# Output projection in two halves of the tokens, in a decoder step on one Trainium2 core

## The chip, the core and the metric

The kernel runs on one core of a Trainium2 chip. The core has a matrix engine (TensorE, PE in the profile; PEld is its weight load), VectorE (DVE), ScalarE (ACT), GpSimd (POOL) and a queue engine that starts transfers (SyncE, SP). They run side by side and wait for each other by semaphores. SBUF is the working memory with 128 partitions, PSUM the memory of eight banks into which TensorE writes. The metric is the device time of one execution in microseconds (us).

## What is computed

One layer of a decoder trunk for 512 prompt tokens and 64 sample tokens (8 sequences of 8), 576 in all, with model width 2048, in float32. Cut to the part that matters here:

```python
h = modulate(rmsnorm(x, norm1_g), shift1, scale1)
proj = h @ w_in                       # five groups of 1024 columns
out_lru = rec * gelu(y_gate)          # recurrent branch
out_sc = sc_b * conv_out              # short convolution
mix = concat([rmsnorm(out_lru, gnorm_lru_g), rmsnorm(out_sc, gnorm_sc_g)]) @ w_out
x = x + gate1 * mix
h2 = modulate(rmsnorm(x, norm2_g), shift2, scale2)
x = x + gate2 * peer(h2)              # 8 heads; queries are h2 @ w_q, 256 columns each
y = rmsnorm(x, final_g)
```

shift, scale and gate come from `silu(c) @ w_ada + b_ada`. `peer` scores the queries against two sets of 128 keys, picks 16 of 16384 experts for each token and head, and sums the chosen rows.

## The kernel before

Activations lie transposed: 128 channels on the partitions, 16 slices of channels (`KD`), 576 tokens (`T`) along the free dimension. A float32 product is made of three: both operands are split into a high part (rounded to the matrix format) and a low part (the rest), and high by high, high by low and low by high are summed in PSUM (`mm3`, L132). The tokens are taken in two moving operands of 288 (`HT`): `movs[0]` holds the first 288 prompt tokens, `movs[1]` the other 224 and the 64 samples. `hv[0]` and `hv[1]` are the high and low parts of the activation.

A weight matrix of 128 output channels comes in two halves of eight slices (`half_w`, L123): a transfer of 512 KB, a copy on ACT that makes the high part, a subtraction that makes the low part. `lo_engine` (L114) gives the subtraction to POOL or VectorE in a fixed share of eighths; all calls before use 8 of 8, so POOL. High, low and raw tiles have two buffers each.

The order on TensorE is written out by hand (`manual_schedule`) through the first part of the kernel; the order on the other engines is planned when the kernel is built, by priority in order of the program and a model of durations.

The stages around the change: The short-convolution branch ends with `sc_b` for its last group; the first eight slices of the mix (recurrent branch) are split into `hv` already. `out_half(0, 0)` and `out_half(1, 0)` take the first eight slices for output tiles 0 and 1, with the second branch's norm statistics (`norm_stats`, `spread`) between and behind. VectorE then norms slices 8 to 15 (L607) and they are split. The loop over `k` (L618) makes the 16 output tiles: product, `x1 = gate * p + x` (L626 to L629, x loaded again as `xk`), a store of x1 to DRAM for the end of the kernel, the sum of squares (`square_sum`), and x1 times scale2 in place (L632, L633), which has to wait until the store has read x1. `ada_turn` puts pieces of the adaLN product (`ada_mm`, one 1 MB tile of `w_ada`, four buffers in `adap`, tag `wa`) between; `ada_out` transposes a finished group.

Behind the loop: the statistics of x1, their spread over partitions by a product (`R`), and for each quarter `q` of the channels `modulate` (L263), which makes h2 in high and low parts, the first query product `mm3(pq0, ...)` for these four slices, and a transposition of the prompt tokens of h2 by products with the identity into `wide`, copied by ACT and stored to `h2d` (L670). Then the other queries follow, with scores and top-16 selection.

PSUM: `pp` has two tiles of two banks (one bank for each token half of an output tile); `pa` and `pst` have two banks each. Behind the loop they are closed, and `ps2` and `psw` take the banks.

Of the kernel before, what the change touches and what calls it, by code (L numbers as in the profile page):

```python
# [81 lines left out]
def build(ctx, tc, A, O, dbg=None):  # L82
# [40 lines left out]
    def half_w(src, nm, hf, share=8):  # L123
        raw = ws.tile([128, 8, 128], F32, name=f"raw_{nm}_{hf}", tag="wraw", bufs=2)
        nc.sync.dma_start(raw, src[:, 8 * hf:8 * hf + 8, :])
        hi = ws.tile([128, 8, 128], F32R, name=f"whi_{nm}_{hf}", tag="whi", bufs=2)
        S.activation(hi, raw, AF.Copy)  # L127
        lo = ws.tile([128, 8, 128], F32R, name=f"wlo_{nm}_{hf}", tag="wlo", bufs=2)
        lo_engine(share).tensor_sub(lo, raw, r32(hi))  # L129
        return hi, lo  # L130

    def mm3(outs, his, los, movs, ks=range(KD)):  # L132

        for k in ks:
            wh, wl = his[k // 8][:, k % 8, :], los[k // 8][:, k % 8, :]
            for st, pick in ((wh, 0), (wh, 1), (wl, 0)):
                first = k == 0 and st is wh and pick == 0
                last = k == KD - 1 and st is wl
                for o, mv in zip(outs, movs):
                    PE.matmul(o, st, mv[pick](k), start=first, stop=last)  # L140
# [24 lines left out]
    pp = p1p.enter_context(tc.tile_pool(name="pp", bufs=2, space=PSUM))  # L165
# [452 lines left out]
    for k in range(KD):  # L618
        if k < 2:
            out_half(k, 1)  # L620
            p = p_out[k]
        else:
            p = project(A["w_out"][k], f"o{k}")
        xk = wk.tile([128, T], F32, name=f"xk{k}", tag="yg", bufs=2)
        nc.sync.dma_start(xk, A["xt"][:, k, :])
        V.scalar_tensor_tensor(x1[:, k, :HT], p[:, 0, :HT], g1[:, k, 0:1], xk[:, :HT], op0=ALU.mult, op1=ALU.add)  # L626
        V.scalar_tensor_tensor(x1[:, k, HT:NP], p[:, 1, :NX], g1[:, k, 0:1], xk[:, HT:NP], op0=ALU.mult, op1=ALU.add)
        V.tensor_tensor(s3(p[:, 1, NX:HT]), s3(p[:, 1, NX:HT]), ctx_b(g1, k), op=ALU.mult)
        V.tensor_add(x1[:, k, NP:], p[:, 1, NX:HT], xk[:, NP:])  # L629
        nc.sync.dma_start(x1d[:, k, :], x1[:, k, :])  # L630
        square_sum(x1[:, k, :], k, st, "n2")
        S.activation(x1[:, k, :NP], x1[:, k, :NP], AF.Copy, scale=mods[4][:, k, 0:1])  # L632
        V.tensor_tensor(s3(x1[:, k, NP:]), s3(x1[:, k, NP:]), ctx_b(mods[4], k), op=ALU.mult)  # L633
        ada_turn(1, 6)
    w_q = stream_w(A["wq"][0], "q00")
    ada_turn(2, 0)
    spread = norm_stats(st, D, "n2")
    ada_turn(1, 0)
    R = spread()
# [4 lines left out]
    psum["p"] = ctx.enter_context(tc.tile_pool(name="ps2", bufs=1, space=PSUM))

    def pbank(tag, nm, bufs):
        return psum["p"].tile([128, 512], F32, name=nm, tag=tag, bufs=bufs)

    psw = ExitStack()
    wp = psw.enter_context(tc.tile_pool(name="psw", bufs=1, space=PSUM))  # L650
# [3 lines left out]
    pq0 = [pbank("u", f"qa00{i}", 2)[:, :HT] for i in range(2)]  # L654
    for q in range(4):
        modulate(x1, R, None, 3, 4 * q, 4, "h2")
        mm3(pq0, *w_q, movs, range(4 * q, 4 * q + 4))
        t = adap.tile([128, 4, 512], F32, name=f"h2s{q}", tag="wa")
        for i in range(NA // 128):
            if i % 2 == 0:  # L660
                wide = wp.tile([128, 2, 512], F32, name=f"wide{q}{i}", tag="wide", bufs=2)
            for k in range(4):
                for p in range(2):
                    PE.matmul(wide[:, i % 2, k * 128:(k + 1) * 128], hv[p][:, 4 * q + k, i * 128:(i + 1) * 128], idr,
                              start=p == 0, stop=p == 1)
            if i % 2:
                with tc.high_priority():
                    S.activation(t[:, i - 1:i + 1, :], wide, AF.Copy)
        for i in range(NA // 128):
# [1272 lines left out]
```

## Time and profile before

| | us |
|---|---|
| three executions | 3202.97, 3201.39, 3187.74 (median 3201.39) |
| the profiled execution | 3192.57 |
| its span, first to last instruction | 3190.7 |
| granted TensorE clock in it, mean | 0.984 of full |
| output projection, densest part | 723.4 to 910.2 us of the span |
| from its last product to the end of the first query product and the turning of h2 | 910.2 to 963.5 us |

The page gives busy times of engines over the span. A row of the timeline gives a start, a duration, the engine, the line, the operation, what is written and read, and in brackets how long the engine sat idle before and who ended that. A row of the windows gives for a stretch the busy time of PE, PEld, DVE, ACT and POOL with instruction counts, the granted clock, and the share and rate of the DMA engines. The first number of a row of a group is its count, then busy us and mean ns.

### The profile page before, as it was taken

What the parts mean: (1) busy time and instruction counts of PE and PEld (TensorE: products, weight loads), DVE (VectorE), ACT (ScalarE), POOL (GpSimd) and SP (SyncE); (2) the same over time, 40 slices, a digit from 0 to 9 for tenths busy, and PEclk for the clock granted to TensorE, in tenths of its full rate; (3) what the DMA queues carried; (4) which work ended last, traced back from release to release, by engine and by line L of the source; (5) the groups of instructions that cost most, each with busy time, mean ns of one, the idle gap of its engine ahead of it and who ended that gap; (6) DMA issues with size and microseconds to landing.
All of it is one profiled execution on the core that took longest, in us unless ns stands there. A gap on an engine that the chain in (4) does not pass through costs nothing.

```text
span 3190.7 us, 46633 instructions
## 1 busy us (share of the span) xinstructions
PE 3063.3 (96%) x17239; PEld 2604.8 (82%) x17239; DVE 2151.6 (67%) x3267; ACT 1045.4 (33%) x1640; POOL 1708.0 (54%) x1001
## 2 busy tenths in 40 slices
PE   6999999999989999999999999998999999999997
PEld 2788888889979998887888788886888888777776
DVE  3455521142245897977898999856677888788755
ACT  3244311122232232232655555542322222222122
POOL 2233333344334235666666666656767777768642
PEclk9999999999999999999999999999999999999998
DMA  9744566633332227889879898989999999899964
GB/s 391 279 137 138 177 215 215 205 121 132 130 121 90 70 83 247 307 312 399 339 309 402 354 400 354 403 281 357 395 376 383 401 341 367 329 397 344 368 245 155
DMA packets 297067, 882.84 MB, mean 277 GB/s; under 512 B 37590, under 2 KB 79446, under 8 KB 245366
## 3 DMA queue, kind: packets, MB, share of 16 engines
q1 hardware_dynamic: 160608, 380.39, 34.0%
q0 software_dynamic: 66336, 413.41, 32.5%
q10 hardware_dynamic: 69888, 86.00, 7.6%
q8 instruction: 136, 2.23, 0.3%
q14 instruction: 99, 0.81, 0.1%
HBM read 879.89 MB, written 66.81 MB: 297 GB/s over the span
## 4 chain that ended last, share of the span: by engine, by line
PE 74%; DMA 12%; DVE 5%; POOL 3%; issue 3%; ACT 1%; SPq 0%; ACTq 0%; POOLq 0%; DVEq 0%
PE pu L1405 20%; PE pv L1425 19%; PE pp_o L140 6%; DMA raw<-v 3%; PE pp_c L140 3%; PE pp_s L140 3%; PE qa L140 3%; PE pp_b L140 3%; PE qb L140 3%; DMA gsb<-gd 3%; PE pp_x L140 2%; PE pp_y L140 2%; PE ada L190 2%; PE gbank L1605 2%; DMA v<-v,rows 2%
## 5 line engine op out<-in xcount | busy, mean ns | idle before, releaser
L909 POOL TENSOR_TENSOR xlo<-raw,xhi 128x1024 fp32r<-128x1024 f32 x320 | 778.6, 2444 | 408.7 <-ACT xhi L908 403.0
L908 ACT ACTIVATE xhi<-raw 128x1024 fp32r<-128x1024 f32 x320 | 338.1, 1060 | 875.4 <-PE pv L1425 319.8
L1263 DVE SCALAR_TENSOR_TENSOR u<-u,hT 128x2048 f32<-128x2048 f32 x223 | 503.7, 2282 | 111.3 <-DMA u<-u,rows 110.0
L1290 DVE SCALAR_TENSOR_TENSOR accB<-v,dots,accB 128x2048 f32<-128x2048 f32 x211 | 496.5, 2353 | 109.4 <-DMA v<-v,rows 103.2
L1425 PE MATMUL pv<-ahi,xhi 128*128 128x512 f32 x1280 | 511.5, 400 | 23.1 <-ACT xhi L908 16.2
L1405 PE MATMUL pu<-hhi,xhi 128*128 128x512 f32 x1280 | 514.4, 402 | 0.0
L1425 PE MATMUL pv<-ahi,xlo 128*128 128x512 f32 x1280 | 508.3, 397 | 4.3 <-POOL xlo L909 4.3
L1425 PE MATMUL pv<-alo,xhi 128*128 128x512 f32 x1280 | 506.0, 395 | 0.0
L1405 PE MATMUL pu<-hhi,xlo 128*128 128x512 f32 x1280 | 502.7, 393 | 0.4 <-POOL xlo L909 0.3
L1405 PE MATMUL pu<-hlo,xhi 128*128 128x512 f32 x1280 | 502.9, 393 | 0.0
L1235 POOL DMA_INDIRECT u<-u,rows x223 | 224.8, 1008 | 211.1 <-DVE u L1263 142.4
L1425 PEld LDWEIGHTS pv<-ahi,xhi 128*128 128x128 f32 x1280 | 243.2, 190 | 80.5 <-ACT xhi L908 17.5
L1425 PEld LDWEIGHTS pv<-ahi,xlo 128*128 128x128 f32 x1280 | 243.1, 190 | 63.0 <-POOL xlo L909 6.2
L1425 PEld LDWEIGHTS pv<-alo,xhi 128*128 128x128 f32 x1280 | 243.6, 190 | 55.2
L1235 POOL DMA_INDIRECT v<-v,rows x223 | 258.1, 1157 | 54.7 <-issue 39.5
L1405 PEld LDWEIGHTS pu<-hhi,xlo 128*128 128x128 f32 x1280 | 240.8, 188 | 56.2 <-POOL xlo L909 2.1
L1405 PEld LDWEIGHTS pu<-hhi,xhi 128*128 128x128 f32 x1280 | 241.4, 189 | 49.4 <-issue 0.9
L1405 PEld LDWEIGHTS pu<-hlo,xhi 128*128 128x128 f32 x1280 | 241.5, 189 | 48.4
L1599 ACT ACTIVATE op<-op,it 128x128 f32<-128x128 f32 x512 | 155.3, 389 | 35.6 <-DVE op L1591 32.8
L1605 PEld LDWEIGHTS gbank<-wr,op 128*128 128x128 f32 x1024 | 133.5, 192 | 24.0 <-ACT stg L1612 15.0
L129 POOL TENSOR_TENSOR wlo_o<-raw_o,whi_o 128x1024 fp32r<-128x1024 f32 x32 | 77.6, 2425 | 119.7 <-ACT whi_o L127 119.7
L1447 DVE TENSOR_TENSOR acc<-acc,pv 128x512 f32<-128x512 f32 x144 | 96.4, 681 | 65.7 <-PE pv L1425 63.6
(498 smaller groups left out, 5439.4 us busy)
## 6 DMA issues: line engine op xcount, KB each, us to landing
wa<-w_ada SPq DMA_DIRECT2D x96, 1024.0 KB
raw<-ut SPq DMA_DIRECT2D x160, 512.0 KB
raw<-v SPq DMA_DIRECT2D x320, 256.0 KB
actd<-act ACTq DMA_DIRECT2D x80, 256.0 KB
gd<-stg ACTq DMA_DIRECT2D x64, 320.0 KB
gsb<-gd ACTq DMA_DIRECT2D x80, 256.0 KB
actr<-actd ACTq DMA_DIRECT2D x40, 512.0 KB
raw_o<-w_out SPq DMA_DIRECT2D x32, 512.0 KB
```

Source lines behind the costliest of these rows:

```text
L129: lo_engine(share).tensor_sub(lo, raw, r32(hi))
L140: PE.matmul(o, st, mv[pick](k), start=first, stop=last)
L908: S.activation(hi, raw, AF.Copy)
L909: G.tensor_sub(lo, raw, r32(hi))
L1235: G.indirect_dma_start(out=out, out_offset=None, in_=src, in_offset=bass.IndirectOffsetOnAxis(ap=idx, axis=0), bounds_check=NE * 128 - 1, ...
L1263: V.scalar_tensor_tensor(r, r, 1.0, st["h"], op0=ALU.mult, op1=ALU.mult, accum_out=dots[i][:, j:j + 1])
L1290: V.scalar_tensor_tensor(st["a"], r, dots[i][:, j:j + 1], st["a"], op0=ALU.mult, op1=ALU.add)
L1405: PE.matmul(pu, st[:, kk, :], movA[mv](k), start=k == 0 and a == 0, stop=k == KD - 1 and a == 2)
L1425: PE.matmul(pv, st, mv, start=first and j == 0 and a == 0, stop=last and not end and j == SG - 1 and a == 2)
L1447: V.tensor_add(ak, ak, pv)
L1599: S.activation(ops[:, j0 + j, :], ops[:, j0 + j, :], AF.Copy, scale=it[2][:, b * 4 + j:b * 4 + j + 1])
L1605: PE.matmul(pg[:, j * L:(j + 1) * L], ops[:, j0 + j, :], wr[:, j0 + j, :], start=True, stop=True)
```

## The change

Each output tile is made twice, once for each half of the tokens: a loop `a` over the halves outside, the loop over `k` inside. One PSUM bank holds one output tile for one half, so the two tiles of `pp` hold four output tiles at a time. All weights of `w_out` are loaded and split twice; from output tile 4 of the first half on, both weight halves come in one 1 MB transfer into an `adap` buffer (`whole`). The subtraction has the share 4 of 8 for the first and 6 of 8 for the second weight half. Since `lo_engine` counts its calls, from output tile 4 on VectorE has the first and POOL the second.

The sum of squares, rsqrt and spread are made for each half (`half_sum`, `half_stats`, `half_spread`), all sums on VectorE. During the second half's loop the first half's statistics are spread (k = 0 and 1) and its h2 is made in four batches of four slices (`half_modulate(0, ...)` at k = 2, 5, 8, 11), multiplications on VectorE. Behind the loop TensorE does the first query product for the first half, then the second half's statistics and the remaining adaLN products, then turns the first 256 prompt tokens of h2, and then, per quarter, the query product of the second half and the other 256 tokens. `pp` moves to the other side of PSUM, so that `ps2` can take its banks while `pa` and `pst` live on, and pools wait tile by tile.

```diff
-    def out_half(k, hf):
-        hi, lo = half_w(A["w_out"][k], f"o{k}", hf)
-        mm3([p_out[k][:, i, :HT] for i in range(2)], (hi, hi), (lo, lo), movs, range(8 * hf, 8 * hf + 8))
+    def out_bank(k, a):
+        if (k, a) not in p_out:
+            t = pp.tile([128, 2, 512], F32, name=f"pp_o{k}_{a}", tag="pp")
+            p_out[k, a], p_out[k + 1, a] = t[:, 0, :HT], t[:, 1, :HT]
+        return p_out[k, a]
+    def out_half(k, hf, a, whole=False):
+        if whole and hf == 0:
+            raw_o[0] = adap.tile([128, 4, 512], F32, name=f"raw_o{k}_{a}", tag="wa")
+            nc.sync.dma_start(raw_o[0], A["w_out"][k].rearrange("p (g k) c -> p g (k c)", g=4))
+        if whole:
+            raw = raw_o[0][:, 2 * hf:2 * hf + 2, :].rearrange("p g (k c) -> p (g k) c", c=128)
...
+            S.activation(hi, raw, AF.Copy)
...
+            lo_engine(6 if hf else 4).tensor_sub(lo, raw, r32(hi))
+        else:
+            hi, lo = half_w(A["w_out"][k], f"o{k}_{a}", hf, 6 if hf else 4)
+        mm3([out_bank(k, a)], (hi, hi), (lo, lo), movs[a:a + 1], range(8 * hf, 8 * hf + 8))
+
+    out_half(0, 0, 0)
+    out_half(1, 0, 0)
     spread = norm_stats(st, W, "g1")
-    out_half(1, 0)
+    out_half(2, 0, 0)
+    out_half(3, 0, 0)
     R = spread()
...
+    def half_modulate(a, k0, mul):
+        t0, n = a * HT, NP - HT if a else HT
+        kk = slice(k0, k0 + 4)
+        for k in range(k0, k0 + 4):
+            m = wk.tile([128, HT], F32, name=f"m_h2{a}_{k}", tag="m2", bufs=2)[:, :n]
+            hi, lo = hv[0][:, k, t0:t0 + n], hv[1][:, k, t0:t0 + n]
+            mul(k).tensor_mul(m, x1[:, k, t0:t0 + n], RT[:, t0:t0 + n])
+            S.activation(hi, m, AF.Identity, bias=sh2[:, k, 0:1])
+            V.scalar_tensor_tensor(lo, m, sh2[:, k, 0:1], r32(hi), op0=ALU.add, op1=ALU.subtract)
+        if a:
...
+    for a in range(2):
+        for k in range(KD):
+            whole = a > 0 or k > 3
+            if whole:
+                out_half(k, 0, a, True)
+            out_half(k, 1, a, whole)
...
+            half_sum(a, k)
+            S.activation(x1[:, k, t0:t0 + n], x1[:, k, t0:t0 + n], AF.Copy, scale=mods[4][:, k, 0:1])
+            if a:
+                V.tensor_tensor(s3(x1[:, k, NP:]), s3(x1[:, k, NP:]), ctx_b(mods[4], k), op=ALU.mult)
+                if k == 0:
+                    cA = half_stats(0)
+                if k == 1:
+                    half_spread(0, cA)
+                if k >= 2 and k % 3 == 2 and k < 12:
+                    half_modulate(0, 4 * (k // 3), lambda k: V)
+            ada_turn(1 - a, 6)
+    w_q = stream_w(A["wq"][0], "q00", 4)
...
+    mm3(pq0[:1], *w_q, movs[:1])
+    cB = half_stats(1)
     while todo or pend:
         ada_turn(4, 0)
+    half_spread(1, cB)
...
+    for q in range(4):
+        half_modulate(1, 4 * q, lambda k: G if k % 3 == 1 else V)
+        turn_rows(q, 0)
+    for q in range(4):
+        mm3(pq0[1:], *w_q, movs[1:], range(4 * q, 4 * q + 4))
+        turn_rows(q, 1)
```

`turn_rows(q, a)` turns the tokens 256 a to 256 a + 255 of quarter q, copies them by ACT and stores two rows of blocks.

More of the change, by code (lines that the diff above doesn't have):

```diff
@@ L164, in build @@
     p1p = ExitStack()
[L165 removed]
+    ppx = ExitStack()
+    pp = ppx.enter_context(tc.tile_pool(name="pp", bufs=2, space=PSUM, side="right"))
     pa = p1p.enter_context(tc.tile_pool(name="pa", bufs=1, space=PSUM))
@@ L615, in build @@
     x1 = big.tile([128, KD, T], F32, name="x1", tag="big")
-    st = []
     g1 = mods[2]
[L618 to L621, printed above, removed]
-        else:
[L623 to L639, printed above, removed]
+    RT = wk.tile([128, T], F32, name="R_n2", tag="R", bufs=1)
+    def half_stats(a):
+        o_ = a * HT
+        pc = pa.tile([128, 3], F32, name=f"pc_n2{a}", tag="pm")
+        for i, x in enumerate((0, 128, HT - 128)):
+            PE.matmul(pc[:, i:i + 1], RT[:, o_ + x:o_ + x + 128], ones[:, 0:1], start=True, stop=True)
+        c = wk.tile([128, 3, 3], F32, name=f"rc_n2{a}", tag="rc", bufs=1)
+        rstd(c[:, 0, :], pc, D, c[:, 1, :], c[:, 2, :])
+        return c
@@ new lines, in half_spread @@
+    def half_spread(a, c):
+        o_ = a * HT
+        pr = pst.tile([128, 512], F32, name=f"st_n2{a}", tag="st")
+        for i in range(2):
+            PE.matmul(pr[:, i * 128:(i + 1) * 128], c[:, 0, i:i + 1].to_broadcast([128, 128]), ident, start=True, stop=True)
+        PE.matmul(pr[:, 256:HT], c[:, 0, 2:3].to_broadcast([128, 128]), ident[:, 512 - HT - 128:], start=True, stop=True)
+        S.activation(RT[:, o_:o_ + HT], pr[:, :HT], AF.Copy)
+    sh2 = mods[3]
+    def half_modulate(a, k0, mul):
[8 more added lines that the diff above has]
+        if a:
+            ms = wk.tile([128, 4, NB * NS], F32, name=f"ms_h2_{k0}", tag="ms", bufs=1)
+            eng = V if k0 < KD // 2 else G
+            eng.tensor_mul(ms, x1[:, kk, NP:], RT[:, None, NP:].to_broadcast([128, 4, NB * NS]))
+            eng.tensor_tensor(s4(ms), s4(ms), ctx_b(sh2, kk), op=ALU.add)
+            split(hv[0][:, kk, NP:T], hv[1][:, kk, NP:T], ms, eng)
@@ L640, in build, with pbank @@
+    w_q = stream_w(A["wq"][0], "q00", 4)
+    ppx.close()
+    psum = {}
+    psum["p"] = ctx.enter_context(tc.tile_pool(name="ps2", bufs=1, space=PSUM, side="right", reuse_waits="tile"))
+    def pbank(tag, nm, bufs):
+        return psum["p"].tile([128, 512], F32, name=nm, tag=tag, bufs=bufs)
+    pq0 = [pbank("u", f"qa00{i}", 2)[:, :HT] for i in range(2)]
+    mm3(pq0[:1], *w_q, movs[:1])
+    cB = half_stats(1)
     while todo or pend:
         ada_turn(4, 0)
+    half_spread(1, cB)
     p1p.close()
-    psum = {}
@@ L644, in build @@
[L644 to L647 removed]
     psw = ExitStack()
[L650 removed]
+    wp = psw.enter_context(tc.tile_pool(name="psw", bufs=1, space=PSUM, reuse_waits="tile"))
     idr = wk.tile([128, 512], F32, name="idr", tag="part", bufs=1)[:, :128].bitcast(F32R)
     V.tensor_copy(idr, ident)
[L654 removed]
@@ L655, in build, with turn_rows @@
[L655 to L661, printed above, removed]
+    rows2 = {}
+    def turn_rows(q, a):
+        if a == 0:
+            rows2[q] = adap.tile([128, 4, 512], F32, name=f"h2s{q}", tag="wa")
+        t = rows2[q]
+        wide = wp.tile([128, 2, 512], F32, name=f"wide{q}{a}", tag="wide", bufs=2)
+        for i in range(2 * a, 2 * a + 2):
@@ L665, in build @@
                               start=p == 0, stop=p == 1)
[L666 to L669, printed above, removed]
+        with tc.high_priority():
+            S.activation(t[:, 2 * a:2 * a + 2, :], wide, AF.Copy)
+        for i in range(2 * a, 2 * a + 2):
             nc.sync.dma_start(h2d[i * 128:(i + 1) * 128, q * 512:(q + 1) * 512], t[:, i, :])
+    for q in range(4):
[4 more added lines that the diff above has]
+        turn_rows(q, 1)
     pe1.close()
```

22 lines of the change are left out of this document (20 added, 2 removed).

## The prediction

> **What bounds the kernel now.** I read the page first, then the table of windows around the output projection, then the timeline at its two ends.
>
> ```profile
> span 3190.7 us, 46633 instructions
> PE 3063.3 (96%) x17239; PEld 2604.8 (82%) x17239; DVE 2151.6 (67%) x3267; ACT 1045.4 (33%) x1640; POOL 1708.0 (54%) x1001
> ```
>
> TensorE (PE) is busy 96% of the span, so work taken off another engine is worth nothing unless PE waited for it. The projection fills 723 to 910 us. The columns are window, its length, then busy us of PE, PEld, DVE, ACT and POOL, the granted clock, and the DMA share and rate.
>
> ```profile
> 692.40:699.40 7.00, 6.61 (x50) 6.37 (x48) 6.23 (x7) 2.32 (x3) 3.40 (x2) 1.00 0.40 142
> 711.60:723.40 11.80, 9.11 (x48) 7.83 (x48) 10.98 (x13) 4.96 (x9) 3.65 (x2) 0.86 0.12 42
> 723.40:910.20 186.80, 186.80 (x1401) 185.76 (x1400) 44.28 (x86) 51.77 (x60) 73.61 (x32) 1.00 0.40 134
> 910.20:926.60 16.40, 9.60 (x78) 4.86 (x77) 11.52 (x25) 7.33 (x13) 5.17 (x3) 0.93 0.51 178
> 926.60:963.50 36.90, 32.62 (x226) 32.16 (x224) 20.63 (x25) 18.12 (x24) 16.56 (x12) 0.85 0.29 100
> ```
>
> In 723 to 910 PE has no gap and 1392 projection matmuls: 185.8 us after 1.0 us of one adaLN product, 0.1335 us each. One weight half (8 k by 3 products by 2 token halves, 48 matmuls) is 6.4 us; with one token half it is 3.2 us. PEld has as many instructions as PE: weights are loaded for each matmul already, so the split by tokens adds no load. The loss lies behind: from 910.2 to 963.5, 53.3 us.
>
> ```profile
> 910.21 1.92 PE L190 MATMUL ada<-wa,cpad 128*32 128x512 f32 x16
> 914.26 1.28 PE L229 MATMUL pc_n<-ones,sqa_n 128*128 128x1 f32 x10 [2.13 <-DVE sqa_n L221]
> 917.43 1.16 PE L237 MATMUL st_n<-ident,rc_n 128*128 128x128 f32 x8
> 918.69 2.78 PE L190 MATMUL ada<-wa,cpad 128*32 128x512 f32 x24
> 925.80 1.11 PE L200 MATMUL pm<-ident,part 128*128 128x128 f32 x4 [4.32 <-ACT part L193]
> 926.56 0.83 PE L140 MATMUL qa<-hhi,whi_q 128*128 128x288 f32 x2
> 945.05 0.47 PE L664 MATMUL wide<-idr,hhi 128*128 128x128 f32 x1 [3.99 <-ACT h2s L668]
> 959.89 0.22 PE L664 MATMUL wide<-idr,hhi 128*128 128x128 f32 x1
> 963.29 0.28 PE L664 MATMUL wide<-idr,hlo 128*128 128x128 f32 x1
> 964.68 0.40 PE L140 MATMUL qb<-hhi,whi_q 128*128 128x288 f32 x1 [1.11 <-ACT h2s L668]
> 967.57 0.44 PE L140 MATMUL qb<-hlo,whi_q 128*128 128x288 f32 x1
> 969.11 0.29 PE L140 MATMUL qb<-hhi,whi_q 128*128 128x288 f32 x1
> ```
>
> And of the other engines:
>
> ```profile
> 919.26 0.69 DVE L284 TENSOR_TENSOR m_h<-x,R_n 128x512 f32<-128x512 f32 x1 [2.10 <-ACT R_n L240]
> 949.54 1.99 DVE L286 SCALAR_TENSOR_TENSOR hlo<-m_h,mod,hhi 128x512 fp32r<-128x512 f32 x1 [0.79 <-ACT hhi L285]
> ...
> 925.17 0.57 ACT L193 ACTIVATE part<-ada 128x512 f32<-128x512 f32 x1
> ```
>
> The first query product starts 16.4 us after the projection ends: sums of squares, rsqrt, spread, the last adaLN products. Then VectorE makes h2 for 32.3 us (919.26 to 951.53) and PE follows it piece by piece. The last 32 turning matmuls take 3.5 us (959.89 to 963.57): 0.11 us each, 14 us for 128. With 96 query matmuls at 0.1335 us (12.8 us), the stage holds 26.9 us of PE work in 36.9 us.
>
> **The change, part by part.** The two ends of a unit first (timeline of several engines):
>
> ```profile
> 860.03 2.40 POOL L129 TENSOR_TENSOR wlo_o<-raw_o,whi_o 128x1024 fp32r<-128x1024 f32 x1 [4.01 <-ACT whi_o L127]
> 861.27 1.77 DVE L221 TENSOR_TENSOR sqa_n<-sqa_n,sq_n 128x576 f32<-128x576 f32 x1 [0.75 <-ACT sq_n L220]
> 862.70 0.72 ACT L632 ACTIVATE x<-x,mod 128x512 f32<-128x512 f32 x1 [1.45 <-DMA x1d<-x]
> 871.70 1.06 ACT L127 ACTIVATE whi_o<-raw_o 128x1024 fp32r<-128x1024 f32 x1 [5.34 <-PE pp_o L140]
> 871.72 0.42 PE L140 MATMUL pp_o<-hhi,whi_o 128*128 128x288 f32 x2
> 871.92 0.52 DVE L626 SCALAR_TENSOR_TENSOR x<-pp_o,mod,xk 128x288 f32<-128x288 f32 x1 [8.73 <-PE pp_o L140]
> 872.83 2.40 POOL L129 TENSOR_TENSOR wlo_o<-raw_o,whi_o 128x1024 fp32r<-128x1024 f32 x1 [4.01 <-ACT whi_o L127]
> ```
>
> The groups and the single lines of code (mean, or shortest/median/longest, in ns):
>
> ```profile
> L129 POOL TENSOR_TENSOR wlo_o<-raw_o,whi_o 128x1024 fp32r<-128x1024 f32 x32 | 77.6, 2425 | 119.7 <-ACT whi_o L127 119.7
> L789 DVE TENSOR_TENSOR oh<-i,f 128x1024 f32<-128x1024 f32 x16 | 20.5, 1283 | 0.1
> ...
> L221 DVE TENSOR_TENSOR sqa_n<-sqa_n,sq_n x24: 757/1232/1774, 10.5 to 912.5; 128x576 f32<-128x576 f32 x24
> L284 DVE TENSOR_TENSOR m_h<-x,R_n x11: 682/686/1649, 919.3 to 948.1; 128x512 f32<-128x512 f32 x11
> L286 DVE SCALAR_TENSOR_TENSOR hlo<-m_h,mod,hhi x32: 739/750/1992, 50.4 to 949.5; 128x512 fp32r<-128x512 f32 x32
> ```
>
> *1. Splits.* Every weight is loaded and split twice: 64 halves for 32, one each 3.2 us. The new shares send a pair's first half to VectorE and its second to POOL (the first four output tiles apart). The split tiles have two buffers, so a half's split starts when PE has done the half before last. That chain is the ACT copy, 1.06 us, 0.07 us (871.70 + 1.06 to 872.83), and POOL's 2.40 us. With one moving operand the copy starts some 0.1 us after the next half's first matmul, so the low part is ready 3.63 us after it, plus some 0.1 us to PE. PE wants it for its third matmul, 3.2 + 0.27 us after. It is late by about 0.3 us once a pair: 31 POOL halves, **+9.3 us**. Before, 6.4 us covered this chain; that cover is gone. Ends: 0 (if the release comes earlier) and 0.45 each, +14. On VectorE the subtraction is taken as the 1.28 us of the equal form of line 789; it leaves 1.2 us in hand. The 32 loads more, of 128x1024 f32 or 0.5 MB (16 MB), add some 80 GB/s to the 134 GB/s of that window, at a DMA share of 0.40, and the whole tiles have four buffers, so I cost it at nothing. The copy that waits for the stored x1 (862.70) stands before the next high part in ACT's queue: about 0.5 us in hand.
>
> *2. The head.*
>
> ```profile
> 692.45 0.42 PE L140 MATMUL pp_o<-hhi,whi_o 128*128 128x288 f32 x2
> 693.46 3.61 DVE L247 TENSOR_TENSOR hlo<-o,hhi 128x576 fp32r<-128x576 f32 x2
> 699.43 1.28 PE L229 MATMUL pc_g<-ones,sqa_g 128*128 128x1 f32 x10 [0.42 <-DVE sqa_g L221]
> ```
>
> The first output tile now goes through its eight slices of the mix in 3.2 us, where it took 6.4. It would reach the seventh at 692.45 + 2.4 = 694.9, but VectorE has that slice's low part at 697.07: PE waits 2.2 us, and the statistics (699.43) come behind it. Two of the four early subtractions also go to a busy VectorE, off a busy POOL. I take **+2 us** (0 to +6: the early split standing behind the 3.61 us). From 711.6 to 723.4 VectorE's second norm paces PE, and under it lie now 24 matmuls, not 48: **+3.2 us** later.
>
> *3. h2 beside the second half.* Per slice VectorE has one multiply and one subtraction, 288 wide for 512: about 0.42 and 0.46 us from 0.686 and 0.750, 14 us for 16. A second-half unit leaves VectorE (about 2 us of sums, 1.28 us of split in 6.5) some 3 us, so four batches of 3.5 us nearly fit. Where a batch stands before a split in VectorE's queue, the split passes its 1.2 us and PE waits. **+3 us**, four times 0.8 (0 to +14: nothing fits).
>
> *4. The joint.* From the last projection matmul: 48 query matmuls on the first half, 6.4; the low part late as above, 0.3; three of five statistics products, 0.8; two adaLN products, 1.9; their copy (0.57, at 925.17) and transposes with the hand-offs, 1.4; two more, 1.9; makes 12.7. The last two want buffers that the first two free at 8.5 and 9.4.
>
> ```profile
> 911.34 0.38 SPq L186 DMA_DIRECT2D wa<-w_ada  x1
> ```
>
> Before, that load was used within 8.4 us of issue (911.34 to the second of three products from 918.69). At 6.5 us they end at 17.0; copy and transposes 1.4, spread 0.9: 19.3. Turning the first half needs nothing of the second: 64 at 0.11 us, 7.0, and 2 us for half rate after a thin stretch. Then 48 query and 64 turning matmuls, 13.4: 41.7 us for 53.3, **-11.6 us**. VectorE's part runs beside: 224 wide for 512, 14 us by width, 18 with the samples, 19.9 to 38 where PE wants the last slice at 38.3. Ends: 35.7 (no late load, no half rate) and 55.6 (h2 as slow as its 32.3 us).
>
> The row at 967.57 shows 0.44 us for a matmul of 0.29, after a wait of 1.11 us: half rate after a short gap. [...]
>
> *5. The tail.*
>
> ```profile
> 970.99 0.41 ACT L931 ACTIVATE qt<-qa 128x288 f32<-128x288 f32 x1 [6.36 <-DMA h2d<-h2s]
> ```
>
> The first query copy waits for the last stores of h2. Behind the last turn there are now two stores, not four, so PE's later wait for it, some 1.3 us, may go: **-1.3 us** (0 to -3).
>
> **Sum:** 9.3 + 2 + 3.2 + 3 - 11.6 - 1.3 = **+4.6 us**. The profiled execution took 3192.57 us and would take 3197.2. The other runs are 3202.97, 3201.39 and 3187.74; the four average 3196.2, their median run is 5 us above that. I set the forecast at 3196.2 + 4.6, **3201 us**: no change that can be told, 0.5% being 16 us.
>
> **Rivals.** *The splits keep up* (0.30): without the 9.3, the 2 and the 3 us, the sum is -9.7 us: 3186; with the joint at its lower end and the tail at -3 it is -17.4: 3179. For it: POOL sat idle 4 us of each 6.4 before its subtraction; against: that idle time was a wait for ACT, and the chain is latency.
>
> *VectorE and POOL take turns* (0.20). The add at 861.27 took 1.77 us where its shortest is 0.757, and ended 0.61 us after POOL's subtraction did. If the 32 h2 operations meet POOL's subtraction, which fills 2.4 of 6.5 us, each batch holds up VectorE's splits by its whole 3.5 us instead of 0.8: 4 times 2.7 more, +15 in all: 3212; with 14 us in place of 9.3 at the splits and 5 in place of 2 at the head, 3219. It decides once a batch runs over the 1.2 us in hand at the split. [...]
>
> *Not beside at all* (0.05). VectorE's order is planned when the kernel is built; if h2's first half lands behind the loop, 14 us stand before the query product, less the 3: 3212.
>
> **How the numbers follow.** The forecast has 0.45, with -6 to +13 us of its own: 3190 to 3209. Faster by over 0.5% needs -16, which only the lower end of the first rival gives, and it would need the late load gone: 0.12. Slower by over 0.5% takes most of the second and third: 0.18. The rest, 0.70, is within. The range for 8 in 10 goes from 3180 to 3220.
>
> **What would show it.** Right: in the loop PE waits some 0.3 us for POOL's low part once in 6.4 us, the stage from the head to the last projection matmul is about 17 us longer; the joint falls from 53.3 to about 42 us, with one gap at an adaLN load. Wrong on the first step: no PE wait on POOL, and a kernel some 10 us faster. Wrong on the third: waits of 2 us or more on VectorE's low part after output tiles 2, 5, 8 and 11. Wrong on the fourth: PE waiting for h2's second half.

## The result and the profile after

| | before | after |
|---|---|---|
| executions, us | 3202.97, 3201.39, 3187.74, 3197.45 (median 3199.42) | 3234.64, 3223.51, 3246.36, 3236.17 (median 3235.40) |
| profiled execution, us | 3192.57 | 3234.64 |
| its span, us | 3190.7 | 3232.8 |

After to before is 1.0111, 95% interval 1.0081 to 1.0140: the change makes the kernel slower by 1.1%, some 36 us by the medians. The forecast was 3201 us in a range of 3180 to 3220, so the prediction was wrong.

The span and the row of busy times of the page of after:

```profile
span 3232.8 us, 46974 instructions
PE 3081.8 (95%) x17243; PEld 2614.1 (81%) x17243; DVE 2248.4 (70%) x3355; ACT 1087.9 (34%) x1721; POOL 1694.1 (52%) x998
```

PE's busy time grew by 18.5 us and the span by 42.1, so PE also waits more. Three stages are compared throughout, each from one row of the timeline to another: the **loop**, from the start of the first output's epilogue (`x1 = gate * p + x`) to the start of the last's; the **stage behind it**, from there to the first copy of a query (`qt<-qa` on ACT); and both together. The ends of after:

```profile
723.97 0.52 DVE L697 SCALAR_TENSOR_TENSOR x<-pp_o,mod,xk 128x288 f32<-128x288 f32 x1 [1.00 <-PE pp_o L140]
...
948.70 0.45 DVE L697 SCALAR_TENSOR_TENSOR x<-pp_o,mod,xk 128x224 f32<-128x224 f32 x1 [1.02 <-PE pp_o L140]
...
1008.99 0.41 ACT L1017 ACTIVATE qt<-qa 128x288 f32<-128x288 f32 x1 [7.02 <-DMA h2d<-h2s]
```

Before, these rows stood at 723.60, 910.32 and 970.99. The loop grew from 186.7 to 224.7 us, the stage behind went from 60.7 to 60.3. The head lost 0.4 us. So up to the first copy of a query the two profiled executions differ by 38.0 us. All of it is lost in the loop, and behind the loop, where 12.9 us were to be gained, only 0.4 us were. (The other 4.1 us of the longer span come later, most of them behind 1550 us, where the differences between two of these traces go up and down by some us.) The windows of after for the loop, for its stretch with the h2 batches, and from the last product to the end of turning (columns as in the prediction):

```profile
724.00:948.70 224.70, 202.40 (x1436) 194.48 (x1430) 139.93 (x173) 95.75 (x140) 71.98 (x30) 0.97 0.55 181
835.95:875.94 39.99, 31.27 (x200) 30.62 (x199) 30.01 (x56) 18.92 (x34) 9.61 (x4) 0.83 0.40 136
948.70:1001.00 52.30, 44.56 (x292) 39.24 (x292) 21.40 (x49) 20.78 (x37) 13.94 (x14) 0.80 0.39 137
```

Where PE had no gap in 187 us, it is now idle for 22 us of the loop, and the granted clock is down where h2 is made. The idle time shows at the start of every second output (timeline of after, VectorE and PE, an early pair and a late one):

```profile
758.03 0.52 DVE L697 SCALAR_TENSOR_TENSOR x<-pp_o,mod,xk 128x288 f32<-128x288 f32 x1 [1.37 <-PE pp_o L140]
758.69 0.37 PE L140 MATMUL pp_o<-hhi,whi_o 128*128 128x288 f32 x1 [0.70 <-DVE x L697]
...
912.55 0.22 DVE L700 TENSOR_TENSOR x<-pp_o,xk 128x64 f32<-128x64 f32 x1
912.92 0.38 PE L140 MATMUL pp_o<-hhi,whi_o 128*128 128x288 f32 x1 [1.16 <-ACT whi_o L613]
```

The second output's first product starts when the epilogue of the output before it has ended: 758.55 and 758.69, 912.77 and 912.92. (For the second wait the view names ACT, whose copy of a high part ended at the same time. But POOL only began the low part that belongs to this copy at 912.86, and PE already used a low part at 913.26: PE works with the weight half before, and the copy is not what it waited for.) The two outputs are the halves of one PSUM tile of two banks, `t[:, 0]` and `t[:, 1]` in `out_bank`. Fifteen second outputs wait like this, 21.0 us together (waits of after in the loop: total, times and longest):

```profile
PE pp_o L140 <- DVE x L700: 9.4, 3, 5.7
PE pp_o L140 <- ACT whi_o L613: 8.1, 7, 1.2
PE pp_o L140 <- DVE x L697: 3.5, 5, 0.7
```

Before, none did, because a tile held the two token halves of one output, finished together. Where h2's batches stand on VectorE, the same wait is long (timeline of after):

```profile
842.68 0.29 PE L140 MATMUL pp_o<-hhi,wlo_o 128*128 128x288 f32 x1
848.69 0.58 PE L140 MATMUL pp_o<-hhi,whi_o 128*128 128x288 f32 x1 [5.72 <-DVE x L700]
...
845.31 0.45 DVE L697 SCALAR_TENSOR_TENSOR x<-pp_o,mod,xk 128x224 f32<-128x224 f32 x1
845.67 2.23 DVE L668 TENSOR_TENSOR m_h<-x,R_n 128x288 f32<-128x288 f32 x1
847.83 0.22 DVE L699 TENSOR_TENSOR pp_o<-pp_o,mod 128x64 f32<-128x64 f32 x1
847.97 0.44 DVE L668 TENSOR_TENSOR m_h<-x,R_n 128x288 f32<-128x288 f32 x1
848.33 0.21 DVE L700 TENSOR_TENSOR x<-pp_o,xk 128x64 f32<-128x64 f32 x1
...
845.15 2.44 POOL L615 TENSOR_TENSOR wlo_o<-raw_o,whi_o 128x1024 fp32r<-128x1024 f32 x1 [5.74 <-ACT whi_o L613]
```

The product ended at 843.0, but its epilogue stood in VectorE's queue behind and between pieces of h2 until 848.54. One of these pieces, a multiply that takes 0.44 us at 847.97, took 2.23 us at 845.67, beside POOL's subtraction (845.15 to 847.59): some 1.8 of the 5.7 us come from there.

Behind the loop (timeline of after):

```profile
957.99 1.24 SPq L187 DMA_DIRECT2D wa<-w_ada  x2
963.15 1.06 PE L191 MATMUL ada<-wa,cpad 128*32 128x512 f32 x8 [1.14 <-DMA wa<-w_ada]
966.87 1.07 PE L191 MATMUL ada<-wa,cpad 128*32 128x512 f32 x8 [2.65 <-DMA wa<-w_ada]
970.99 0.41 ACT L657 ACTIVATE R_n<-st_n 128x288 f32<-128x288 f32 x1 [2.33 <-PE st_n L656]
...
985.96 0.55 PE L140 MATMUL qa<-hhi,whi_q 128*128 128x288 f32 x1
1000.63 0.28 PE L744 MATMUL wide<-idr,hlo 128*128 128x128 f32 x1
```

The late adaLN loads were issued at 957.99 and the last was there at 966.87; the spread ended at 971.4; the first half's turning took until 985.96 and the rest until 1000.9: 52.4 us after the last product at 948.5, where it was 53.3 before.

### The profile page after: what moved, and what is told of

Its sections match the earlier page's. It is cut to its first block, busy times and chain, and to the rows that moved or that the text cites. A ratio compares the mean times of both kernels' runs of the same rounds, so it can differ in the third digit from the quotient of the medians.

```text
span 3232.8 us, 46974 instructions
## 1 busy us (share of the span) xinstructions
PE 3081.8 (95%) x17243; PEld 2614.1 (81%) x17243; DVE 2248.4 (70%) x3355; ACT 1087.9 (34%) x1721; POOL 1694.1 (52%) x998
## 3 DMA queue, kind: packets, MB, share of 16 engines
q8 instruction: 136, 2.23, 0.3%
## 4 chain that ended last, share of the span: by engine, by line
PE 41%; DMA 13%; POOL 7%; issue 5%; DVE 3%; ACT 1%; SPq 0%; POOLq 0%; ACTq 0%; DVEq 0%
PE pv L1511 17%; PE pu L1491 15%; DMA gsb<-gd 6%; POOL xlo L995 4%; PE qa L140 3%; POOL u L1321 3%; PE qb L140 3%; DMA raw<-v 2%; DMA actr<-actd 1%; DMA v<-v,rows 1%; PE gbank L1691 1%; DMA u<-u,rows 1%; DVE u L1349 1%; PE sc L830 0%; PE pv L1515 0%
## 5 line engine op out<-in xcount | busy, mean ns | idle before, releaser
L1321 POOL DMA_INDIRECT u<-u,rows x223 | 224.3, 1006 | 212.0 <-DVE u L1349 148.4
L1511 PEld LDWEIGHTS pv<-ahi,xhi 128*128 128x128 f32 x1280 | 243.6, 190 | 76.8 <-ACT xhi L994 12.8
L1321 POOL DMA_INDIRECT v<-v,rows x223 | 251.3, 1127 | 54.8 <-issue 38.6
L140 PE MATMUL pp_o<-hhi,whi_o 128*128 128x288 f32 x512 | 156.0, 305 | 25.7 <-DVE x L700 9.4
L140 PE MATMUL pp_o<-hhi,wlo_o 128*128 128x288 f32 x512 | 155.3, 303 | 2.3 <-DVE wlo_o L129 1.0
L140 PE MATMUL pp_o<-hlo,whi_o 128*128 128x288 f32 x512 | 154.6, 302 | 2.1 <-DVE hlo L248 1.8
```

The source lines that it names most:

```text
L1321: G.indirect_dma_start(out=out, out_offset=None, in_=src, in_offset=bass.IndirectOffsetOnAxis(ap=idx, axis=0), bounds_check=NE * 128 - 1, ...
L1511: PE.matmul(pv, st, mv, start=first and j == 0 and a == 0, stop=last and not end and j == SG - 1 and a == 2)
```

## The experiments

Two theories for the loop were tested: A, the shared PSUM tile (the wait for another output's epilogue), and B, the prediction's second rival, that VectorE and POOL take turns and the weights' low parts are late. Other runs change the stage behind the loop. Loop, stage behind and their sum in us, from each run's trace by the rows named above, and the ratio to before. (The ratio goes by executions of before taken beside each run, so it is not the quotient of the medians in this table.)

| run | loop | behind | sum | median | ratio, 95% interval |
|---|---|---|---|---|---|
| before | 186.7 | 60.7 | 247.4 | 3199.42 | |
| after | 224.7 | 60.3 | 285.0 | 3235.40 | 1.0111 [1.0081, 1.0140] |
| e1_own_bank | 206.5 | 59.1 | 265.6 | 3216.66 | 1.0048 [1.0019, 1.0076] |
| e2_ada_in_loop | 225.0 | 49.1 | 274.1 | 3221.70 | 1.0086 [1.0064, 1.0109] |
| e3_h2_behind | 224.3 | 60.2 | 284.5 | 3235.35 | 1.0125 [1.0109, 1.0142] |
| e4_bank_ada | 210.7 | 48.1 | 258.7 | 3211.45 | 1.0053 [1.0033, 1.0072] |
| e5_bank_ada_v | 199.3 | 48.6 | 247.8 | 3197.71 | 1.0013 [0.9995, 1.0032] |
| e7_turn_mixed | 211.7 | 43.2 | 254.9 | 3207.18 | 1.0052 [1.0036, 1.0067] |
| e8_turn_v | 201.6 | 43.2 | 244.7 | 3199.65 | 1.0023 [1.0010, 1.0037] |
| e9_bank_h2_after | 201.4 | 73.5 | 274.9 | 3230.57 | 1.0114 [1.0088, 1.0141] |
| f1_v2 | 200.7 | 38.6 | 239.3 | 3193.71 | 1.0007 [0.9992, 1.0023] |
| f2_inloop | 221.0 | 54.1 | 275.1 | 3225.65 | 1.0101 [1.0083, 1.0120] |
| g1_warm | 210.7 | 53.9 | 264.6 | 3217.64 (one) | |
| f3_cross | 199.8 | 43.9 | 243.6 | 3193.77 | 0.9997 [0.9978, 1.0015] |

Before was run again beside each group; its medians there were 3194.64 to 3197.85. Single executions of one kernel spread by 10 to 15 us to either side, so small steps are read from the stages, each in one execution.

**One tile for each output (e1).**

```diff
-            t = pp.tile([128, 2, 512], F32, name=f"pp_o{k}_{a}", tag="pp")
-            p_out[k, a], p_out[k + 1, a] = t[:, 0, :HT], t[:, 1, :HT]
+            p_out[k, a] = po.tile([128, 512], F32, name=f"pp_o{k}_{a}", tag="po")[:, :HT]
```

`po` is a pool of four tiles of one bank, opened in the place of `pp`. (It also waits tile by tile, `reuse_waits="tile"`, which `pp` does not.)

> Each output tile of the projection gets its own PSUM tile of one bank (four of them) in place of half a tile of two banks shared by outputs k and k+1. Theory A (shared tile): TensorE's first matmul of every second output waits for VectorE's epilogue of the output before it, because both write one PSUM tile; in the changed kernel these starts are late by 0.86 to 1.39 us each, and by 5.9 and 3.1 us where h2's batches stand ahead of the epilogue, about 22 us with the half-rate matmuls behind the long ones counted apart. By A the loop (724 to 949 us, 225 us) falls to 198 to 206 us and the kernel to 3208 to 3217 us. Theory B (VectorE's and POOL's turns): the weights' low parts are late because VectorE's in-order queue and the two engines' turns at SBUF hold up the splits, and the wait on the epilogue is only where it shows; then TensorE waits for low parts instead, the loop stays above 218 us and the kernel within 8 us of 3235.

The loop fell by 18.2 us to 206.5, just above the 198 to 206 of A and far below B's 218; the median, 3216.66 us, is within A's range. What is left (waits of e1 in the loop, total, times and longest; and the end of one such chain in its timeline):

```profile
PEld pp_o L140 <- POOL wlo_o L616: 7.3, 22, 0.4
PEld pp_o L140 <- DVE wlo_o L616: 4.9, 6, 1.0
...
769.52 2.40 POOL L616 TENSOR_TENSOR wlo_o<-raw_o,whi_o 128x1024 fp32r<-128x1024 f32 x1 [4.32 <-ACT whi_o L614]
771.98 0.41 PE L140 MATMUL pp_o<-hhi,wlo_o 128*128 128x288 f32 x1
```

No wait for an epilogue is left. POOL's late low part, the prediction's first term, shows at 22 outputs: subtraction until 771.92, PE at 771.98. So A is the larger part of the loss, but not all: e1's loop is still 19.8 us longer than before's, and late low parts, B's sign, are what PE waits for now (e5 and e9 take this rest apart). The new pool costs something at the head: its first product waits 2.2 us for the banks of the product before, which it did not in after.

**The late adaLN products in the loop (e2).**

```diff
-            ada_turn(1 - a, 6)
+            ada_turn(1 if a == 0 or k >= 10 else 0, 0 if a else 6)
```

> The last six adaLN products are taken one after each of the last six outputs of the second half, in place of all six behind the first query product. Theory: behind the loop the last two loads were issued only when the first two products had freed their buffers (957.99 us) and TensorE waited until 966.87, and the spread of the second half's scale stood behind that; without it the stage from the last projection matmul to the last turning matmul falls from about 52 us by 9 to 13 us, the loop grows by the six products, 5.8 us, and the kernel is 4 to 8 us faster than the changed one (3227 to 3231 us). Rival: VectorE's h2 of the second half and ACT's copies of the turned rows set the pace there anyway; then the stage falls by less than 5 us and the kernel is the same or slower.

The stage behind fell by 11.2 us, as expected. The loop did not grow by the 5.8 us of the products (225.0 for 224.7 us), it seems because they ran where PE would have waited for an epilogue; e4, without these waits, bears this out. So the kernel gained more than forecast (3221.70).

**Both edits, e1's and e2's (e4).**

> Both edits, own PSUM tiles and the adaLN products in the loop. If they are independent their gains add: by theory A 22 to 34 us less than the changed kernel, 3201 to 3213 us, about level with the kernel before. Rival: where the loop is faster, the weights' loads or POOL's late low parts take up what is gained, and it stays above 3215 us.

3211.45 us, in the expected range, near its upper end. The sum of the stages fell by 26.3 us, where e1 and e2 alone gave 19.4 and 10.9: with no epilogue to wait for, the products cost the loop 4.1 us.

**h2 behind the loop (e3, e9).** In e3 the four batches only stood later in the source, in e9 also the spread that they need:

```diff
-                if k == 1:
-                    half_spread(0, cA)
-                if k >= 2 and k % 3 == 2 and k < 12:
-                    half_modulate(0, 4 * (k // 3), lambda k: V)
...
+    half_spread(0, cA)
+    for q in range(4):
+        half_modulate(0, 4 * q, lambda k: V)
```

> The first half's h2 is made behind the loop, ahead of the first query product, in place of in four batches beside the second half; the shared PSUM tiles stay. Theory A (shared tile): the loop loses what the batches add to the epilogue (5.9 and 3.1 us for 1.3 each, some 6 us, and 4 to 5 us of half rate behind them), 10 to 12 us, and keeps the waits of 0.9 to 1.3 us at every second output; behind the loop some 14 us of VectorE's work come to stand on the path: the kernel is 0 to 6 us slower than the changed one. Theory B (VectorE and POOL): the loop's second half falls to about 105 us from 121, all its waits gone with the batches.

e3 tells nothing on this: the planned order left the batches in the loop, with the same waits of 5.7 and 2.9 us, so its time is the changed kernel's once more (3235.35 and 3235.40 us). e9, on top of e1:

> Own PSUM tiles as in e1_own_bank, and the spread of the first half's scale stands behind the loop, so that its h2 cannot be made before (in e3_h2_behind only the order in the source was changed, and the planned order of VectorE was the same, with the batches in the loop). This prices 'beside the second half' by itself. Theory: once the epilogue holds up nobody, the batches cost the loop 3 to 5 us: 206.5 us falls to 201.5 to 204; behind the loop 14 to 18 us of VectorE's work come on the path, so the kernel is 8 to 16 us slower than e1_own_bank. Rival: the batches cost the loop 10 us or more even with own tiles; then the loop falls below 198 us and the kernel is within 6 us of e1_own_bank.

The loop fell from 206.5 to 201.4 us and the stage behind grew by 14.4; the kernel is 13.9 us slower than e1, as expected. With own tiles, h2 beside the second half costs the loop 5.1 us, and it hides 14.

**All low parts on VectorE (e5, on top of e4).**

```diff
-            lo_engine(6 if hf else 4).tensor_sub(lo, raw, r32(hi))
+            V.tensor_sub(lo, raw, r32(hi))
```

> Own PSUM tiles and adaLN products in the loop as in e4_bank_ada, and all low parts of the split projection on VectorE (1.23 us each) in place of every second on POOL (2.40 us). Theory A: what is left in the loop is POOL's chain of copy and subtraction, 0.25 to 0.30 us and a second step of 0.11 at each of some 27 outputs, 10 us in all; on VectorE the chain is 2.4 us and ends before TensorE's third matmul; and VectorE's other work gets shorter, since its adds (2.3 to 2.4 us beside POOL's subtraction, 0.45 alone) lose their partner. The loop falls from 210.7 us to 199 to 204, the kernel to 3200 to 3206 us. Rival: VectorE is full where h2's batches run, 3.5 us each beside two splits of 1.23, and waits of over 1 us come back at the low parts there; then the loop stays above 207 us.

The loop fell by 11.4 us to 199.3, and the window of e5's loop shows PE without gaps although six products are in it; VectorE, with 28 splits more, is busy for 119.4 us where it was 137.8 in e4. The reason is in the add of the sums of squares (groups of that line: shortest, median and longest ns; after first, then e5):

```profile
L685 DVE TENSOR_TENSOR R_n<-R_n,sq_n x30: 444/2290/2472, 730.5 to 950.2; 128x288 f32<-128x288 f32 x30
```

```profile
726.30:925.60 199.30, 199.00 (x1484) 191.33 (x1488) 119.36 (x202) 96.61 (x141) 4.77 (x2) 0.99 0.65 215
...
L686 DVE TENSOR_TENSOR R_n<-R_n,sq_n x30: 448/450/2490, 733.3 to 927.6; 128x288 f32<-128x288 f32 x30
```

Beside POOL's subtraction an add of 0.45 us takes 2.3. The rival (VectorE full at the batches) is refuted. At 3197.71 us the kernel is below what was expected, and the loss against before is gone within the interval.

**The stage behind (e7, e8, f1, g1, f2, f3).** In e4 the first half's turning ran at half rate (windows of e4, during it and after the next products):

```profile
949.20:959.60 10.40, 10.40 (x51) 10.29 (x49) 9.45 (x21) 5.78 (x14) 3.89 (x5) 0.50 0.13 50
...
966.20:979.00 12.80, 12.78 (x106) 12.64 (x105) 2.05 (x6) 7.42 (x10) 3.11 (x2) 1.00 0.63 215
```

e7 (on top of e4) mixes it with the query product, ahead of the norm; e8 is e7 with e5's splits:

```diff
+        for i in range(2 * a, 2 * a + 2):
+            wide = pbank("g", f"wide{q}{i}", 2)
...
+            mm3(pq0[a:a + 1], *w_q, movs[a:a + 1], range(4 * q + 2 * (i % 2), 4 * q + 2 * (i % 2) + 2))
...
+    turn_rows(0, 0)
+    cB = half_stats(1)
+    turn_rows(1, 0)
+    half_spread(1, cB)
```

> Own PSUM tiles, adaLN products in the loop (from the tenth output on), splits as in the change. Behind the loop the turning of the first half is mixed with the first half's query product, eight turning matmuls and six query matmuls at a time, into single banks, ahead of the second half's norm, in place of query product, norm, then 64 turning matmuls in a row. In e4_bank_ada those 64 took 0.213 us each, at a granted clock of 0.50, for 15 us. Theory: the clock stays at 1.0 when turning is mixed with query matmuls, and the norm's waits are filled: the stage from the last epilogue of the projection to the first query copy falls from 48.1 us to 34 to 40 us and the kernel to 3198 to 3205 us. Rival: VectorE's 19 us of h2 for the second half set the pace; then TensorE only waits for them instead, and the stage stays above 44 us.

> All four edits: own PSUM tiles, adaLN products in the loop, all low parts of the projection on VectorE, and the first half's turning mixed with its query product. If the gains of the two kernels before it add, the stage from the first epilogue to the first query copy, 258.7 us in e4_bank_ada and 247.4 in the kernel before, falls to 235 to 244 us and the kernel is 3 to 12 us faster than before: 3185 to 3194 us. Rival: the gains overlap or VectorE becomes the bound; then it is within 3 us of before or slower.

Both fell short: the stage took 43.2 us, neither the 34 to 40 expected nor the rival's 44, and e7's median, 3207.18, is above what was expected. The sum in e8 is 2.7 us below before's, but the median is above before's (1.0023): the rival's outcome, not the 3 to 12 us of gain. PE waits for copies that stand behind high parts of h2 in ACT's queue (timeline of e8):

```profile
950.29 0.42 ACT L247 ACTIVATE hhi<-ms_h 128x256 fp32r<-128x256 f32 x1 [1.09 <-POOL ms_h L676]
950.61 0.58 ACT L737 ACTIVATE h2s<-wide 128x512 f32<-128x512 f32 x1
951.25 0.47 PE L734 MATMUL wide<-idr,hhi 128*128 128x128 f32 x1 [2.42 <-ACT h2s L737]
```

ACT was waiting for POOL's samples (`ms_h`, the sample tokens of h2) while the copy stood behind. f1 takes POOL out of h2's second half:

```diff
-            eng = V if k0 < KD // 2 else G
+            eng = V
...
-        half_modulate(1, 4 * q, lambda k: G if k % 3 == 1 else V)
+        half_modulate(1, 4 * q, lambda k: V)
```

> e8_turn_v, and two more edits: h2's second half is made by VectorE alone, samples too (POOL had five slices' multiplies and two batches' samples); and the output tiles' ring of banks starts two banks on, so that the first tile does not wait for the banks that the last product before it still held (2.2 us at 696.8 us). Theory: ACT's in-order queue stood with the copies of the turned rows behind the high parts whose multiply POOL was late with; without POOL the waits for these copies (1.0, 2.4 and 0.5 us) and the half rate behind them go, and the stage from last epilogue to first query copy falls from 43.2 us to 35 to 39; with the 2 us at the head the kernel is 0 to 6 us faster than before. Rival: VectorE's own work for the half, some 19 us, sets the pace and the stage stays above 41 us.

The stage fell to 38.6 us, as expected. The two banks left out of the ring had no effect: PE still waited 2.2 us for the first tile. The sum is 8.1 us below before's, yet the kernel only equals it (1.0007, 0.9992 to 1.0023), where 0 to 6 us of gain were expected. The two traces show where the gain goes, by the same instruction in a later stage (timelines of before, then of f1):

```profile
1385.99 0.69 DVE L1083 CAST words<-i 128x512 uint32<-128x512 f32 x1
...
1382.24 0.69 DVE L1169 CAST words<-i 128x512 uint32<-128x512 f32 x1
```

The loop starts 1.8 us later than before's, so at the first copy of a query f1 is 6.3 us ahead, at this row 3.8 and at the end of the span 1.3. g1 is e4 with 30 matmuls of no use, which take 5.6 us themselves:

```diff
+    for _ in range(30):
+        PE.matmul(pq0[1], w_q[0][0][:, 0, :], movs[0][0](0), start=True, stop=True)
```

> e4_bank_ada, with 30 matmuls more between the second half's spread and the 64 turning matmuls of the first half: all the same product of 128x288 (first slice), into the bank of the second half's query product, which its real first product overwrites. They add work and compute nothing that is used. Question: in e4_bank_ada the 64 turning matmuls ran at a granted clock of 0.50 for 15 us without a gap of over 0.3 us but one, and the clock came back 1.8 us after the first 128x288 matmul. Theory: turning matmuls (128x128, each with its own weight load) do not bring the clock back, matmuls of 128x288 do, and turning keeps it once it is at 1.0: the 30 take 5 to 6 us, the first dozen at half rate, the turning then takes 0.11 us each for 0.213, and the stage from last epilogue to first query copy is 43 to 49 us. Rival: the turning lets the clock fall again by itself; then it takes 0.213 us each as before and the stage is 52 us or more.

53.9 us is the rival's time, but not for its reason (one execution). The first 32 turning matmuls ran at 0.11 us each, as the theory said; then PE waited 2.4 us for a copy on ACT, and the clock was at half again (g1: windows, timeline):

```profile
959.00:963.00 4.00, 2.62 (x24) 2.48 (x23) 3.56 (x7) 2.13 (x6) 2.63 (x4) 0.95 0.00 0
963.00:967.00 4.00, 3.00 (x14) 3.00 (x15) 2.16 (x5) 2.11 (x5) 2.88 (x5) 0.50 0.34 131
...
957.94 0.22 PE L745 MATMUL wide<-idr,hhi 128*128 128x128 f32 x1
964.00 0.47 PE L745 MATMUL wide<-idr,hhi 128*128 128x128 f32 x1 [2.38 <-ACT h2s L748]
```

So the half rate was not the only bound there: behind the full rate stood ACT's copies. f2 puts the first half's turning into the loop, in the tiles of the norm's spread, behind outputs 12 to 15, and the last adaLN products from output 3 on:

```diff
+            ada_turn(1 if a == 0 or 3 <= k else 0, 0 if a else 6)
+            if a and k > 11:
+                turn_rows(k - 12, 0)
```

> f1_v2, but the first half's turning stands in the loop behind its last four outputs (in the banks of the norm's spread), and the last adaLN products one per output from the fourth on; behind the loop the query product of the first half alone runs beside the norm. Theory: TensorE's work is the same, and the loop grows by the 7.1 us of turning; behind it the second half's h2 sets the pace and the stage falls to 30 to 34 us; the sum is equal to f1_v2 within 3 us. Rival: in the loop the turning fills waits that are there anyway and its copies do not stand behind h2's, so that the sum is 4 us or more shorter than f1_v2.

A miss on both sides: the loop is 221.0 us, and the stage behind took 54.1 us where 30 to 34 were expected. PE waited 7.3, 7.3 and 6.7 us for a high part whose load came late (timeline of f2, the load, ACT and PE of the second time):

```profile
931.19 0.45 SPq L612 DMA_DIRECT2D raw_o<-w_out  x1
937.19 2.00 ACT L616 ACTIVATE whi_o<-raw_o 128x1024 fp32r<-128x1024 f32 x2 [4.08 <-DMA raw_o<-w_out]
938.30 0.61 PE L140 MATMUL pp_o<-hhi,whi_o 128*128 128x288 f32 x1 [7.26 <-ACT whi_o L616]
```

The turned rows use the same four buffers as the weights, and the load of this weight was issued only 7 us before its product; that the shared buffers are the reason is read from the code and not shown, since it was not tried with buffers of their own. f3 is e8 with f1's edit to h2 and, for the tiles, only other partners:

```diff
+            for j in range(2):
+                t = pp.tile([128, 2, 512], F32, name=f"pp_o{k + j}_{a}", tag="pp")
+                p_out[k + j, a], p_out[k + j + 2, a] = t[:, 0, :HT], t[:, 1, :HT]
```

> f1_v2, but in place of a new ring of single banks the change's own tiles of two banks are kept, and only who shares one is changed: outputs k and k+2 in one, k+1 and k+3 in the other. Theory A says that the wait is for the epilogue of the output that shares the tile; with one output of 6.4 us between the two it is long over, so the loop is as in f1_v2, 199 to 203 us; and the first tile no longer waits 2.2 us for the banks of the product before, so the kernel is 2 to 3 us faster than f1_v2, about 3189 to 3194 us, 0.998 to 1.000 of before. Rival: any second writer of a tile of two banks waits, whoever had it; then the loop is above 212 us.

The loop is 199.8 us, as in f1: a shared tile cost nothing here, where the partner's epilogue was an output earlier. This settles A from the other side, and since f3 keeps the pool of the changed kernel, e1's gain does not come from the way its new pool waits. The wait at the head is 1.0 instead of 2.2 us. The stage behind, the same instructions as in f1, took 5.3 us more: the granted clock stayed at 0.50 from 946 to 966 us, where f1 had 1.00 to 960 (see the last section). f3 is level with before (0.9997, 0.9978 to 1.0015), not the 2 to 3 us faster than f1 that were expected. No version was faster than before by more than the measurement tells.

## Why the prediction was wrong

Up to the first copy of a query the sum was +4.6 us and the traces show +38.0. Of the 33.4 us between, 22.5 are in the loop (forecast +15.5: 9.3 of splits, 3.2 of moved matmuls, 3 of h2; measured +38.0), 12.5 in the stage behind it (forecast -12.9, measured -0.4), and the head came out 1.6 us better. The loop by differences of the runs: moved matmuls 3.2 (24 at 0.1335), shared tile 18.2 (after to e1), POOL's low parts 11.4 (e4 to e5), batches 5.1 (e1 to e9): 37.9. Two of these have a second measure. e9's loop, without batches, is 14.7 us longer than before's, 3.2 and 11.5 for POOL's low parts. e5's, without POOL but with batches and with six products of adaLN (5.8 us), is 12.6 longer, which leaves 3.6 for the batches. So the parts are good to some 2 us, and that they add up to within 0.1 us is chance.

- **The step that failed is a missing term.** The prediction followed the chain of the weights (step 1) and VectorE's queue (step 3), and cost the epilogue at nothing. It named what is late next on the side of the low parts, but not who else writes the tile that the epilogue reads. The diff had it: two outputs in `t[:, 0]` and `t[:, 1]`. With the epilogue's 0.52 us (first half) and 0.97 us (second half, 911.80 to 912.77), some 15 starts of 0.7 to 1.2 us could have been put down. The waits in after are 21.0 us, and e1 measures 18.2. With that in the sum the forecast would have been some 3219 us; most of what then is missing is step 4.
- **Step 4 (-11.6) failed in its sizes** and came to -0.9. Point by point from the last product: the first half's query product ended at 7.7 us (forecast 6.7); the last loads were issued at 9.5 (forecast 9.4) but the second was there only some 8 us later, for the 6.5 taken, and PE's part of the spread ended at 22.3 instead of 19.3; the turning took 15.2 us instead of 9, at a granted clock of 0.50 for all of it and with a wait for ACT; the rest 14.9 instead of 13.4. The order was right, and each of the sizes was taken too low, the half rate most of all: 2 us were set for it, and 64 matmuls at 0.213 us for 0.11 are 6.6. e2 shows that the late products with their loads were worth 11.2 us and need not have stood there.
- **Step 1 (+9.3)** was right in kind and about right in size: 22 late low parts in e1 and a loop 11.4 us shorter without POOL, which also frees VectorE. The sign named for it (0.3 us once in 6.4) is there in e1; in after the wait of the second output hid half of them. By the step's own numbers VectorE's low part has 0.9 us in hand (3.47 less 0.1, 1.06, 0.07, 1.28 and 0.1), not 1.2. Of the six that are late in e1, four are at the batches, by 0.5 to 0.8 us.
- **Step 2** was nearly right in size, 3.2 us of matmuls moved and 0.4 us lost at the head for a forecast of 2, but not in its reason. PE did not wait for the slice of the mix: with no POOL subtraction beside them (POOL idle from 689.69 to 693.23) VectorE made the two low parts in 1.41 us, where before they took 3.61, beside one of 2.89 (693.57). It waited 1.03 us for a weight's low part on VectorE, what the step had named for its upper end.
- **Step 3 (+3)** has about the right size by itself, 3.6 to 5.1 us. In the changed kernel the batches cost more, since they also held up the epilogue that the next output waited for: from 835.95 to 875.94, 40.0 us for four outputs, where four others take 29.1 (two of 14.55). The sign that was named, 2 us or more at VectorE's low part, did not come; the wait was at the epilogue.
- **Step 5 (-1.3)** did not come: the copy of the query still waited for the last store, 7.0 us idle for 6.4.
- **The rivals.** "The splits keep up" did not hold: e1 and e5 show the late low parts. "VectorE and POOL take turns" was right that VectorE's adds are held up beside POOL's subtraction (2.29 us for an add of 0.45). Its 3212 to 3219 us contain e1's 3216.66, but by luck: it held some 14 us for the batches, which cost 3.6 to 5.1, and a gain of 12.9 behind the loop, where e1 has 1.6. That the batches land behind the loop did not happen.

What stays open: why the clock stays at half in some stretches behind the loop, and what moves the differences between two traces by some us in the stages behind 1550 us.

## What to carry to other kernels

When a loop's unit is halved, ask of every buffer that it writes who else holds a part of the same tile: in this kernel two units in one tile made the second wait for the first one's reader, and everything queued ahead of that reader then stood on the path. Pair a unit with one that is finished long before, or give each a tile of its own. A product that is off the path in the old order (the last adaLN loads here) should be moved along with the work that covered its load.

## What was not expected of the hardware

The granted clock. The turning matmuls (128x128) of after and e4 stayed at 0.50 for over 10 us without a gap; in e4 the 128x288 matmuls from 964.40 on had 1.00 again from 966.2 (windows of e4 above, of after here).

```profile
970.70:981.20 10.50, 10.50 (x50) 10.36 (x49) 9.47 (x21) 5.81 (x14) 3.88 (x5) 0.50 0.13 50
```

With the two mixed, eight to six, it went either way: f1 and f3 execute the same instructions in the following stretches (windows of f1, then of f3), and e8 ran such a stretch at half from 951.25 to 957.85 at least (starts of turning matmuls 0.21 us apart for 0.11).

```profile
950.00:960.00 10.00, 9.05 (x75) 8.82 (x74) 1.19 (x4) 5.79 (x10) 2.39 (x1) 1.00 0.40 126
```

```profile
950.00:966.00 16.00, 16.00 (x74) 16.00 (x73) 0.65 (x2) 4.59 (x8) 2.38 (x1) 0.50 0.37 131
```

f3 did 16 us of unbroken work at half rate: going on without a gap did not bring the full rate back there. Nor did the length of the gap before decide: f3 fell to half behind a wait of 1.48 us (945.54), f1 kept 1.00 behind one of 1.49 (946.31), and before fell behind 1.11 (964.68). Why f3 fell and f1 did not, one execution of each cannot tell.

VectorE and POOL. Of the 30 adds of sums of squares in after, 26 ran into a subtraction of POOL's; they took 1.42 to 2.47 us, and each ended 0.31 to 0.33 us after the subtraction. The four others took 0.44 or 0.45 us. The median of all 30 is 2.29 us, and 0.45 in e5, where POOL has two subtractions left in the loop. One pair (timeline of after, POOL and VectorE):

```profile
912.86 2.40 POOL L615 TENSOR_TENSOR wlo_o<-raw_o,whi_o 128x1024 fp32r<-128x1024 f32 x1 [4.36 <-ACT whi_o L613]
913.28 2.29 DVE L685 TENSOR_TENSOR R_n<-R_n,sq_n 128x288 f32<-128x288 f32 x1 [0.51 <-ACT sq_n L684]
```

The subtraction ends at 915.26, the add at 915.57. Taking the subtractions off POOL and giving them to VectorE made VectorE less busy in the loop, 119.4 us in e5 for 137.8 in e4.
